# Three chunks of the merge gates as block products behind the recurrent branch, and one plain chunk between each two pairs of the branch

## The chip, the cores and the metric

The kernel runs on one NeuronCore of one Trainium2 chip. The metric is device time in microseconds (us), lower is better; a stated time is the median of several executions. A profile shows one execution. Its engines are TensorE (PE, matrix products), VectorE (DVE), ScalarE (ACT), GpSimd (POOL) and SyncE (SP), which here only issues loads. Each engine runs its instructions in order and waits on semaphores for the others.

## The reference

One layer of a streaming encoder: 512 frames of 1024 features, all in float32.

```python
xn = rmsnorm(h, norm_mix_g)
u = xn @ w_in                       # 1024 x 7168: q, k, v, xr, gr, ga, gb
ya = chunked_band_attention(q, k, v, rel_table) @ w_attn_out
xc = causal_depthwise_conv(xr, conv_w, conv_b)
hr = rg_lru(xc, w_r, b_r, w_i, b_i, lam)
yb = (hr * gelu(gr)) @ w_rnn_out
g_a, g_b = split(sigmoid(concat(ga, gb) + b_merge))
h = h + (g_a * ya + g_b * yb) @ w_o
h = h + SwiGLU(rmsnorm(h)); out = rmsnorm(h)
```

What matters here are the merge gate g_b = sigmoid(xn @ W_gb + b), 512 x 1024, and the branch's way out, yb.

## The kernel before, in words

**Products.** Every float32 operand is split into a high part (float32r) and the low rest; mm3 (L74) makes a product as three matmuls: high x high, high x low, low x high. Weights come in chunks of 256 columns (two tiles of 128 output features, c = 0 and 1). A plain chunk holds two half chunks of four k tiles each; project (L342) runs eight k of three matmuls over 512 frames for each c, that is 48 matmuls of 128 x 512. The weight is the stationary operand, and xn, turned so that features lie on partitions (xnT), moves past it.

**Chunks.** plan (L96) lists the chunks in the order of their use, `xr0 gr0 ga0 gb0 xr2 ...`. weights (L336) hands out a chunk and has prefetch (L308) load and split the ones ahead of it: load (L157) issues the load on SP into a "raw" buffer (three), ScalarE copies the high part (L82), VectorE subtracts it for the low part (L83), both into "whl" buffers (four, so two chunks).

**Block products.** Chunks named in `strassen` (in the feed-forward stage, from chunk 2 on) are multiplied in another form: weight_sums (L181) cuts the chunk in four blocks (two halves of k, two halves of the columns), forms four sums s1 to s4 of blocks on VectorE and splits a11, a12, (s2, s1), (s3, s4) and a22. block_product (L362) then does seven products of four k, over 256 frames each: a11 b11, a12 b21, s2 t2, s1 t1, s3 t3, s4 b22, a22 t4, where b are blocks of the moving side and t1 to t4 its sums. ScalarE keeps partial results (L370), VectorE adds them (L382, L383). That makes 84 matmuls of 128 x 256.

**The stage in question.** Pair by pair (j = 0, 2, 4, 6) the recurrent branch runs: xr, its conv (conv_in, conv_taps, conv_out), gr with GeLU, the small gate matmuls "rg" (L709), then a chain on ScalarE, VectorE and GpSimd (rnn_gates L715, rnn_scan L739) that ends with the tile rnn (L746, L747). Between pairs stand plain chunks of merge gates: after pairs 0 and 2 ga and gb, after 4 and 6 only gb. Each gate tile is half a tanh (L780). Then come q and k of head pair 0, v0 (four v_tile's), yb0 to yb6 (L968 to L972, multiplied into the gate zB), and the heads. The scores of head 0 are asked for before yb6. The heads (transposed, scores, weigh) are in a section whose TensorE order is written out by hand; there transposed turns the probabilities through two PSUM banks "t" and one "mm". PSUM has four banks "mm", two "s" and two "t"; the v tiles of v0 use "t".

**Order.** Outside sections with a manual schedule a list scheduler in the compiler orders each engine's instructions: ready ones first, in the order of the code. Pools of SBUF are stacked; a pool opened after another is closed lies on the same memory, and each of its tiles waits for the tiles that lay there. The branch's pools rw and rw2 are closed ahead of attention's aw2 and aw.

## Time and profile before

| what | value |
|---|---|
| median of 3 executions | 866.96 us (866.88 to 867.3) |
| the profiled execution | 867.3 us |
| its span, first to last instruction | 865.5 us |
| TensorE busy | 856.4 us (99%) |
| VectorE busy | 600.9 us (69%) |
| ScalarE busy | 498.1 us (58%) |
| GpSimd busy | 95.2 us (11%) |
| TensorE's granted clock | 0.998 of full |

"Busy" is the time in which an instruction of the engine ran. Matmuls overlap, so the rate is read from the distance between starts, not from their lengths. In a timeline row the columns are: start, duration, engine, line, operation, output and inputs, shapes, count, and in brackets the idle time before it with what ended it. In a row of groups: line, engine, operation, shapes, count, then total busy us, mean ns, and idle us before with what ended it.

### The profile page before, as it was taken

What the parts mean: (1) busy time and instruction counts of PE and PEld (TensorE: products, weight loads), DVE (VectorE), ACT (ScalarE), POOL (GpSimd) and SP (SyncE); (2) the same over time, 40 slices, a digit from 0 to 9 for tenths busy, and PEclk for the clock granted to TensorE, in tenths of its full rate; (3) what the DMA queues carried; (4) which work ended last, traced back from release to release, by engine and by line L of the source; (5) the groups of instructions that cost most, each with busy time, mean ns of one, the idle gap of its engine ahead of it and who ended that gap; (6) DMA issues with size and microseconds to landing.
All of it is one profiled execution on the core that took longest, in us unless ns stands there. A gap on an engine that the chain in (4) does not pass through costs nothing.

```text
span 865.5 us, 13353 instructions
## 1 busy us (share of the span) xinstructions
PE 856.4 (99%) x5130; PEld 761.1 (88%) x5130; DVE 600.9 (69%) x950; ACT 498.1 (58%) x878; POOL 95.2 (11%) x161
## 2 busy tenths in 40 slices
PE   9999999999999999999999999999999999999997
PEld 6988888888889889898888889999999999888885
DVE  5666656573456585766556556988888888698885
ACT  6595747752356585767633357555555556545434
POOL 2412111120112132221200000000000001000000
PEclk9999999999999999999999999999999999999999
DMA  9133232433323332232223712424333332437542
GB/s 289 57 119 106 68 120 76 123 98 98 109 88 95 81 103 74 81 113 64 74 76 121 266 51 72 145 79 131 109 98 98 99 98 85 148 100 227 185 134 97
DMA packets 88767, 96.39 MB, mean 111 GB/s; under 512 B 5784, under 2 KB 74992, under 8 KB 88704
## 3 DMA queue, kind: packets, MB, share of 16 engines
q1 hardware_dynamic: 87072, 92.03, 34.3%
q10 hardware_dynamic: 1232, 2.95, 0.9%
q8 instruction: 40, 0.66, 0.3%
q0 software_dynamic: 400, 0.57, 0.2%
q14 instruction: 23, 0.19, 0.1%
HBM read 93.39 MB, written 2.14 MB: 110 GB/s over the span
## 4 chain that ended last, share of the span: by engine, by line
PE 97%; DVE 1%; ACT 1%; DMA 0%; issue 0%; ACTq 0%; DVEq 0%
PE po_out L76 2%; PE po_out L77 2%; PE po_out L78 2%; PE o L941 2%; PE p_fu L78 2%; PE p_fg L78 2%; PE p_fg L77 2%; PE p_fg L76 2%; PE p_fu L76 2%; PE p_fu L77 2%; PE pT L921 2%; PE po_v L76 2%; PE po_v L78 2%; PE po_v L77 2%; PE po_gb L76 2%; PE po_xr L77 2%
## 5 line engine op out<-in xcount | busy, mean ns | idle before, releaser
L910 POOL TENSOR_SCALAR p<-p,rl 128x128 f32<-128x128 f32 (+3 forms) x61 | 34.9, 590 | 135.7 <-DVE rl L906 135.4
L905 ACT ACTIVATE p<-p,m 128x128 f32<-128x128 f32 (+1 forms) x64 | 35.7, 560 | 11.0 <-DVE m L904 10.8
L76 PE MATMUL po_v<-whl_v,xnT 128*128 128x256 f32 x128 | 36.5, 285 | 0.0
L78 PE MATMUL po_v<-whl_v,xnT 128*128 128x256 f32 x128 | 36.2, 283 | 0.0
L77 PE MATMUL po_v<-whl_v,xnT 128*128 128x256 f32 x128 | 36.2, 283 | 0.0
L1131 POOL TENSOR_TENSOR act_lo<-act,act_hi 128x1024 fp32r<-128x1024 f32 x1 | 2.4, 2405 | 300.7 <-ACT act_hi L1130 300.7
L76 PE MATMUL po_out<-whl_fo,act_hi 128*128 128x512 f32 (+1 forms) x80 | 30.8, 385 | 0.5 <-ACT c_u L370 0.5
L78 PE MATMUL po_out<-whl_fo,act_lo 128*128 128x512 f32 (+1 forms) x80 | 30.7, 384 | 0.0
L77 PE MATMUL po_out<-whl_fo,act_hi 128*128 128x512 f32 (+1 forms) x80 | 30.7, 384 | 0.0
L904 DVE CUSTOM_DVE_ANT_0 p<-s,bias 128x128 f32<-128x128 f32 (+1 forms) x64 | 29.1, 483 | 1.0 <-PE s L896 1.0
L83 DVE TENSOR_TENSOR whl_qk<-raw_qk,whl_qk 128x1024 fp32r<-128x1024 f32 x16 | 20.5, 1284 | 13.2 <-ACT whl_qk L82 13.0
L83 DVE TENSOR_TENSOR whl_fu_s<-s_fu,whl_fu_s 128x1024 fp32r<-128x1024 f32 x20 | 24.1, 1222 | 6.2 <-ACT whl_fu_s L82 6.2
L77 PE MATMUL po_xr<-xnT,whl_xr 128*128 128x512 f32 (+1 forms) x80 | 27.7, 353 | 0.0
L83 DVE TENSOR_TENSOR pp<-pT,pp 128x384 fp32r<-128x384 f32 (+1 forms) x48 | 27.5, 596 | 0.1
L77 PE MATMUL po_gr<-xnT,whl_gr 128*128 128x512 f32 (+1 forms) x80 | 27.5, 347 | 0.0
L78 PE MATMUL po_gr<-xnT,whl_gr 128*128 128x512 f32 (+1 forms) x80 | 27.3, 347 | 0.0
L78 PE MATMUL po_xr<-xnT,whl_xr 128*128 128x512 f32 (+1 forms) x80 | 27.2, 346 | 0.0
L76 PE MATMUL po_gr<-xnT,whl_gr 128*128 128x512 f32 (+1 forms) x80 | 27.2, 347 | 0.0
L83 DVE TENSOR_TENSOR whl_fg_s<-s_fg,whl_fg_s 128x1024 fp32r<-128x1024 f32 x20 | 24.0, 1222 | 4.1 <-ACT whl_fg_s L82 4.0
L76 PE MATMUL po_xr<-xnT,whl_xr 128*128 128x512 f32 (+1 forms) x80 | 26.3, 351 | 0.4 <-ACT xnT L566 0.4
L82 ACT ACTIVATE whl_qk<-raw_qk 128x1024 fp32r<-128x1024 f32 x16 | 16.8, 1053 | 17.0 <-PE po_yb L78 10.4
L76 PE MATMUL po_gb<-xnT,whl_gb 128*128 128x512 f32 x64 | 25.2, 394 | 0.0
(487 smaller groups left out, 3247.5 us busy)
## 6 DMA issues: line engine op xcount, KB each, us to landing
raw_fg<-in_w_ffn_in_dram SPq DMA_DIRECT2D x24, 512.0 KB, 4.2
raw_fu<-in_w_ffn_in_dram SPq DMA_DIRECT2D x22, 512.0 KB, 3.9
raw_qk<-in_w_in_dram SPq DMA_DIRECT2D x32, 256.0 KB, 3.2
raw_fo<-in_w_ffn_out_dram SPq DMA_DIRECT2D x16, 512.0 KB, 3.6
raw_xr<-in_w_in_dram SPq DMA_DIRECT2D x8, 512.0 KB, 4.3
raw_gr<-in_w_in_dram SPq DMA_DIRECT2D x8, 512.0 KB, 3.6
raw_ga<-in_w_in_dram SPq DMA_DIRECT2D x8, 512.0 KB, 4.7
raw_gb<-in_w_in_dram SPq DMA_DIRECT2D x8, 512.0 KB, 3.5
```

Of the source, the lines that this page charges most:

```text
L76: pe.matmul(o, sh, mh, start=start, stop=False, skip_group_check=parts)
L77: pe.matmul(o, sh, ml, start=False, stop=False, skip_group_check=parts)
L78: pe.matmul(o, sl, mh, start=False, stop=stop, skip_group_check=parts)
L82: act.activation(hi, src, AF.Copy)
L83: dve.tensor_sub(lo, src, f(hi))
L904: dve.tensor_tensor_reduce(prob[qb][:], scs[qb][:, 0:w], bias[:, S - w:S], -1.0, 3e38, ALU.add, ALU.min, nmax[:, qb:qb + 1])
L905: act.activation(prob[qb][:], prob[qb][:], AF.Exp, bias=nmax[:, qb:qb + 1], scale=-1.0, accum_out=lsum[:, qb:qb + 1])
L910: eng.tensor_scalar(prob[qb][:], prob[qb][:], rl[:, qb:qb + 1], 1.0, ALU.mult, ALU.mult)
L921: pe.transpose(pt[:, at * P:(at + 1) * P], prob[qb][:, kb * P:(kb + 1) * P], ident[:])
L941: pe.matmul(po[:, S - n:S], st, pp[i][:, part, lo:lo + n], start=kb == 0 and part == 0, stop=kb == NT - 1 and part == 1)
L1131: (dve if i else pool).tensor_sub(lo[:], o[:], f(hi[:]))
```

## The change

gb0, gb2 and gb4 are computed as block products, at a new place. The order of chunks between the branch's pairs becomes: ga0 after pair 0, ga2 after pair 2, q and k of head pair 0 after pair 4, gb6 after pair 6. Then: yb0, the sums t1 to t4 of xn (sums_of_x), yb2, gb0, yb4, gb2, gb4, yb6, and last v0 and the heads, with head 0's scores ahead of v0. yb0 to yb4 are copied to zB unmultiplied (way_out); block_gate puts its product in a tile of ta that is not yet used, applies the tanh there and multiplies into zB. A pool gs holds the sums between the closing of rw and rw2 and the opening of aw2 and aw; its first 32 KB for each partition are the split sums, then the place for sums in the making. The feed-forward stage keeps its own sums pool, and the counters are reset for it. The diff without the lines that only rename sums_room:

```diff
@@ -91,29 +91,29 @@
 
     chunks = []
     index = {}
-    strassen = [f"f{w}{j}" for j in range(2, FT, 2) for w in "gu"]
+    strassen = ["gb0", "gb2", "gb4"] + [f"f{w}{j}" for j in range(2, FT, 2) for w in "gu"]
 
     def plan(name, *parts, rows=0, kts=KT):
         index[name] = len(chunks)
         chunks.append((name, parts, rows, kts))
+
+    def plan_qk(pr):
+        plan(f"qk{pr}", cols(w_in, C_Q + pr * P, P), cols(w_in, C_K + pr * P, P))
 
     for j in range(0, KT, 2):
         plan(f"xr{j}", cols(w_in, C_XR + j * P))
         plan(f"gr{j}", cols(w_in, C_GR + j * P))
         if j < 4:
             plan(f"ga{j}", cols(w_in, C_GA + j * P))
-        plan(f"gb{j}", cols(w_in, C_GB + j * P))
-
-    def plan_qk(pr):
-        plan(f"qk{pr}", cols(w_in, C_Q + pr * P, P), cols(w_in, C_K + pr * P, P))
+        if j == 4:
+            plan_qk(0)
 
     def plan_v(gr):
         plan(f"v{gr}", cols(w_in, C_V + gr * CW))
 
-    plan_qk(0)
+    for name in ("gb6", "yb0", "yb2", "gb0", "yb4", "gb2", "gb4", "yb6"):
+        plan(name, cols(*((w_in, C_GB + int(name[2]) * P) if name[0] == "g" else (w_rnn_out, int(name[2]) * P))))
     plan_v(0)
-    for j in range(0, KT, 2):
-        plan(f"yb{j}", cols(w_rnn_out, j * P))
     for pr in range(1, HEADS // 2):
         plan_qk(pr)
         if pr in (2, 4, 6):
@@ -160,7 +160,7 @@
         n = min(4 * CW // wide, kts - k)
         at = rows + k * P
         pl, bufs = wp, 3
-        if name in strassen and name[0] == "f":
+        if name in strassen:
             loads[0] += 1
             pl, bufs = (room[0], 1) if loads[0] % 4 == 0 and loads[0] > 4 else (wp, 3)
         raw = pl.tile([P, n, wide], F32, tag="raw", bufs=bufs, name=f"raw_{name}_{k}")
@@ -465,7 +466,7 @@
     gm_p = ps.tile([P, S], F32, tag="s", bufs=2, name="gm_p")
     pe.transpose(gm_p[:, 0:8], gm_r[:], ident[0:8, 0:8])
     gm = cp.tile([P, 8], F32, name="gm")
-    _, xnT = features(xnp, "xn", "xnT")
+    xnT_all, xnT = features(xnp, "xn", "xnT")
 
 
     vc = cp.tile([P, NV], F32, name="vc")
@@ -794,26 +795,10 @@
         g = [gelu_in(0, po[0])]
         xch.append(conv_out(1, xc[1]))
         g.append(gelu_in(1, po[1]))
-        prefetch(index["gb0"] + 1)
+        prefetch(index["xr2"] + 1)
         for c in range(2):
             gelu_out(g[c], po[c])
             conv[c] = xc[c], xch[c], g[c]
-    for j in range(0, KT, 2):
-        if j:
-            for c in range(2):
-                conv[j + c] = rnn_conv(j + c, tile_of(f"xr{j}", c, ahead=2))
-        for c in range(2):
-            if j:
-                po = tile_of(f"gr{j}", c, "t")
-                conv[j + c] += (rnn_gelu(j + c, po),)
-        if j:
-            gates_of(j)
-        for w in range(j // 4, 2):
-            for c in range(2):
-                gate(w, j + c)
-            if j == w == 0:
-                gates_of(j)
-
 
     def blocks(ap):
         return ap.rearrange("p (b i) -> p b i", i=P)
@@ -855,10 +840,83 @@
             pool.tensor_copy(kl[other, e], kl[own, e])
         qk[pr] += [kh, kl]
 
-    q_tile(0)
-    k_tile(0)
+    for j in range(0, KT, 2):
+        if j:
+            for c in range(2):
+                conv[j + c] = rnn_conv(j + c, tile_of(f"xr{j}", c, ahead=2))
+            for c in range(2):
+                po = tile_of(f"gr{j}", c, "t")
+                conv[j + c] += (rnn_gelu(j + c, po),)
+            gates_of(j)
+        if j < 4:
+            for c in range(2):
+                gate(0, j + c)
+        elif j == 4:
+            q_tile(0)
+            k_tile(0)
+        else:
+            for c in range(2):
+                gate(1, j + c)
+        if j == 0:
+            gates_of(0)
+
     rw2_stack.close()
     rw_stack.close()
+
+    gs_stack, gs = opened("gs")
+    bt_homes = {i: gs.tile([P, 2, 4, 256], F32R, name=f"xt{i}") for i in (2, 1, 3, 4)}
+    sums_room[0] = room[0] = gs
+
+    def way_out(j):
+        for c in range(2):
+            po = mm_tile(f"po_yb{j + c}")
+            project(po, weights(f"yb{j}"), c, rnn)
+            act.activation(zB[j + c], po[:], AF.Copy)
+
+    def block_of_x(kh, half, part):
+        return xnT_all[:, 4 * kh:4 * kh + 4, part, half * 256:half * 256 + 256]
+
+    def sums_of_x():
+
+        x32 = gs.tile([P, 2, 4, 256], F32, tag="whl", name="x32")
+        x12, x22 = x32[:, 0], x32[:, 1]
+        t1, t2, t3, t4 = (gs.tile([P, 4, 256], F32, tag=tag, bufs=bufs, name=f"x_t{i + 1}")
+                          for i, (tag, bufs) in enumerate((("s21", 1), ("s34", 1), ("a22", 2), ("a22", 2))))
+        dve.tensor_add(x12, f(block_of_x(0, 1, 0)), f(block_of_x(0, 1, 1)))
+        dve.tensor_sub(t1[:], x12, f(block_of_x(0, 0, 0)))
+        dve.tensor_sub(t1[:], t1[:], f(block_of_x(0, 0, 1)))
+        dve.tensor_add(x22, f(block_of_x(1, 1, 0)), f(block_of_x(1, 1, 1)))
+        dve.tensor_sub(t2[:], x22, t1[:])
+        dve.tensor_sub(t3[:], x22, x12)
+        dve.tensor_sub(t4[:], f(block_of_x(1, 0, 0)), t2[:])
+        dve.tensor_add(t4[:], t4[:], f(block_of_x(1, 0, 1)))
+        for i, t in ((2, t2), (1, t1), (3, t3), (4, t4)):
+            split_pair(bt_homes[i], t[:])
+        return right_side(lambda kh, half, part, k: block_of_x(kh, half, part)[:, k], [bt_homes[i] for i in range(1, 5)])
+
+    def block_gate(j, n, x_right):
+
+
+        z, o = zs[0][2 + n % 2], zs[1][j // 2]
+        block_product(f"gb{j}", n % 2, x_right, z[:].rearrange("p a (b n) -> p (a b) n", n=256))
+        for c in range(2):
+            at = 24 + j + c
+            act.activation(z[:, c], z[:, c], AF.Tanh, bias=hb[:, at:at + 1], scale=0.5)
+        dve.scalar_tensor_tensor(o[:], z[:], 1.0, o[:], ALU.add, ALU.mult)
+
+    way_out(0)
+    x_right = sums_of_x()
+    way_out(2)
+    block_gate(0, 0, x_right)
+    way_out(4)
+    block_gate(2, 1, x_right)
+    block_gate(4, 0, x_right)
+
+    for j in (6, 7):
+        po = mm_tile(f"po_yb{j}")
+        project(po, weights("yb6"), j % 2, rnn)
+        dve.scalar_tensor_tensor(zB[j], zB[j], 1.0, po[:], ALU.add, ALU.mult)
+    gs_stack.close()
     aw2_stack, aw2 = opened("aw2", 2)
     aw_stack, aw = opened("aw", 2, "right")
 
@@ -961,15 +1019,9 @@
                 2: ([va(1), va(2)], [va(3)]),
                 3: ([qs(second)], [ks(second)])}[at]
 
+    prob = scores(0)
     for t in range(NT):
         v_tile(0, t)
-
-    for j in range(KT):
-        if j == 6:
-            prob = scores(0)
-        po = mm_tile(f"po_yb{j}")
-        project(po, weights(f"yb{j - j % 2}"), j % 2, rnn)
-        dve.scalar_tensor_tensor(zB[j], zB[j], 1.0, po[:], ALU.add, ALU.mult)
     with tc.manual_schedule(engines={mybir.EngineType.PE}):
         for h in range(HEADS):
             pp = transposed(h, prob)
@@ -1002,7 +1054,8 @@
 
     hp = ctx.enter_context(pool_of("h", 1, "right"))
 
-    sums_room = ctx.enter_context(pool_of("sums", 1, "right"))
+    sums_room[0] = ctx.enter_context(pool_of("sums", 1, "right"))
+    slots[0] = loads[0] = 0
     hn_stack, hnp = opened("hnT", 1, "right")
     ht = [hp.tile([P, D], F32, name=f"h{t}") for t in range(NT)]
     for t in range(NT):
@@ -1121,10 +1174,10 @@
         if i == 0:
             hi = acp.tile([P, 2, S], F32R, tag="act", bufs=13, name=f"act_hi{i}")
         elif i < 3:
-            hi = sums_room.tile([P, 2, S], F32R, tag=("s21", "s34")[i - 1], bufs=1, name=f"act_hi{i}")
+            hi = sums_room[0].tile([P, 2, S], F32R, tag=("s21", "s34")[i - 1], bufs=1, name=f"act_hi{i}")
         else:
             if i == 3:
-                hi_room.append(sums_room.tile([P, 2, 2, S], F32R, tag="whl", bufs=1, name="act_hi34"))
+                hi_room.append(sums_room[0].tile([P, 2, 2, S], F32R, tag="whl", bufs=1, name="act_hi34"))
             hi = hi_room[0][:, i - 3]
         lo = acp.tile([P, 2, S], F32R, tag="act", bufs=13, name=f"act_lo{i}")
         act.activation(hi[:], o[:], AF.Copy)
```

7 lines of the change are left out of this document (4 added, 3 removed).

## The prediction

> **What bounds the kernel now.** I read the page first: the engine shares, the granted clock, and the chain that ended last.
>
> ```profile
> span 865.5 us, 13353 instructions
> PE 856.4 (99%) x5130; PEld 761.1 (88%) x5130; DVE 600.9 (69%) x950; ACT 498.1 (58%) x878; POOL 95.2 (11%) x161
> ...
> PEclk9999999999999999999999999999999999999999
> ...
> PE 97%; DVE 1%; ACT 1%; DMA 0%; issue 0%; ACTq 0%; DVEq 0%
> ```
>
> TensorE is busy for 99% of the span at full clock, and 97% of the last chain is TensorE itself. So a change pays only by taking matmul time out, and it costs whatever makes TensorE wait. Busy shares hide the rate, because neighbouring matmuls overlap; the timeline gives start-to-start times. First, one chunk of merge gate as it is now, from its first matmul to the first one of the next chunk:
>
> ```profile
> 94.57 0.39 PE L76 MATMUL po_gb<-xnT,whl_gb 128*128 128x512 f32 x1
> ...
> 105.45 0.39 PE L76 MATMUL po_xr<-xnT,whl_xr 128*128 128x512 f32 x1
> ```
>
> The 48 matmuls (two halves, eight k, three each) of 512 columns take 10.88 us, 0.2267 us each. Second, a block product of the feed-forward stage, which has the shape that the gates are to get:
>
> ```profile
> 577.99 0.28 PE L76 MATMUL p_fg<-hn,whl_fg_a 128*128 128x256 f32 x1
> 578.11 0.28 PE L77 MATMUL p_fg<-hn,whl_fg_a 128*128 128x256 f32 x1
> 578.23 0.28 PE L78 MATMUL p_fg<-hn,whl_fg_a 128*128 128x256 f32 x1
> ```
>
> A matmul of 256 columns starts every 0.12 us, a little over half of 0.2267.
>
> **The change part by part.** *The matmuls.* A block product does seven products of four k and three matmuls: 84 x 0.12 = 10.08 us in place of 48 x 0.2267 = 10.88 us. That is 0.80 us less per chunk, and 2.4 us less for gb0, gb2 and gb4. All other matmuls stay and only move. The price per matmul decides: at 10.88 / 84 = 0.1295 us nothing would be gained, and the row shows 0.12.
>
> [...]
>
> *The new order.* gb0 and gb2 leave the branch, and qk0 takes the place of gb4 (24 + 24 matmuls of 512 columns, also 10.88 us). So everything from the last pair of the branch on comes two chunks, 21.76 us, earlier. Behind that pair now come gb6, yb0, yb2, gb0, yb4, gb2, gb4, yb6. The rows that matter are where TensorE is, and when the branch ends:
>
> ```profile
> 161.75 1.66 PE L709 MATMUL rg<-xch,wrg 64*128 64x512 f32 x12
> 163.34 0.50 PE L76 MATMUL po_gb<-xnT,whl_gb 128*128 128x512 f32 x1
> ```
>
> ```profile
> 182.05 1.26 DVE L742 SCALAR_TENSOR_TENSOR u<-u,g 128x512 f32<-128x512 f32 x2
> ...
> 183.53 2.55 POOL L747 TENSOR_TENSOR rnn<-u,rnn 128x512 fp32r<-128x512 f32 x2 [8.71 <-ACT rnn L746]
> ```
>
> The last gate matmuls of the branch (rg) start at 161.75, gb6 at 163.34; the two last rnn tiles are written by 186.08, the first of them at about 184.8. Shifted: gb6 starts at 141.58 and ends at 152.46, the rnn tiles are there at 163.0 and 164.3. Before, gb6, qk0 and v0 covered this; now yb0 follows gb6 and needs rnn6 for its seventh k. If TensorE kept strictly to the order of the code, it would run 18 matmuls (4.08 us, to 156.5) and then stand for 6.5 us. But the first six k of the four tiles of yb0 and yb2 are 72 matmuls or 16.3 us, which reach to 168.8. That the schedule does bring such matmuls forward is seen in the profile of before:
>
> ```profile
> 190.86 0.28 PE L78 MATMUL po_v<-whl_v,xnT 128*128 128x256 f32 x1
> 190.98 0.40 PE L76 MATMUL po_yb<-rnn,whl_yb 128*128 128x512 f32 x1
> ...
> 192.59 0.28 PE L76 MATMUL po_v<-whl_v,xnT 128*128 128x256 f32 x1
> ```
>
> Seven matmuls of yb stand between two of the v tiles, taken forward because v had no bank. The four tiles need four "mm" banks, and there are four. I cost this at nothing, with 4.5 us to spare; without that cover it costs 6.5 us.
>
> *The sums, on VectorE.* gb0's first two products need only raw blocks and x. The third, s2 with t2, needs sums of both. gb0 starts two chunks after gb6's end, at 174.2; 24 matmuls later, at 177.1, s2 and t2 must be there. From 141.6 that is 35.5 us. What VectorE has to do by then, priced by these rows:
>
> ```profile
> L83 DVE TENSOR_TENSOR whl_fg_s<-s_fg,whl_fg_s 128x1024 fp32r<-128x1024 f32 x20 | 24.0, 1222 | 4.1 <-ACT whl_fg_s L82 4.0
> L83 DVE TENSOR_TENSOR whl_fg_a<-raw_fg,whl_fg_a 128x512 fp32r<-128x512 f32 x30 | 20.3, 684 | 1.1 <-ACT whl_fg_a L82 1.0
> L1146 DVE TENSOR_TENSOR act<-act,c_u 128x1024 f32<-128x1024 f32 x10 | 12.2, 1219 | 0.3 <-ACT c_u L370 0.3
> L741 DVE TENSOR_TENSOR_SCAN u<-a,gt 128x512 f32<-128x512 f32 x8 | 9.3, 1208 | 0.0
> L195 DVE TENSOR_TENSOR s_fg<-raw_fg,raw_fg 128x512 f32<-128x512 f32 x10 | 6.9, 687 | 0.2 <-DMA raw_fg<-in_w_ffn_in_dram 0.2
> L735 DVE SCALAR_TENSOR_TENSOR u<-u 128x512 f32<-128x512 f32 x8 | 5.8, 732 | 0.5 <-POOL a L733 0.5
> L731 DVE SCALAR_TENSOR_TENSOR u<-gt,u 128x512 f32<-128x512 f32 x8 | 5.6, 698 | 8.0 <-ACT gt L729 8.0
> L736 DVE SCALAR_TENSOR_TENSOR gt<-gt,xc 128x512 f32<-128x512 f32 x8 | 5.5, 693 | 14.0 <-ACT gt L721 14.0
> L697 DVE SCALAR_TENSOR_TENSOR g<-g,po_gr 128x512 f32<-128x512 f32 x8 | 5.5, 686 | 2.7 <-ACT g L696 2.7
> L740 DVE SCALAR_TENSOR_TENSOR gt<-gt,u 128x512 f32<-128x512 f32 x8 | 5.2, 688 | 3.0 <-ACT u L759 3.0
> L742 DVE SCALAR_TENSOR_TENSOR u<-u,g 128x512 f32<-128x512 f32 x8 | 5.2, 675 | 0.0
> ```
>
> The branch's last pair: 2 x (0.693 + 0.698 + 0.732 + 0.688 + 1.208 + 0.675) = 9.4, and 1.4 for what is left of its GeLU. Weights of yb0 and yb2: 4 x 1.22 = 4.9. Sums of x: eight of 1024 elements at 1.22 = 9.8. The low parts of the four sums: 4 x 1.22 = 4.9. gb0: four sums at 0.69, two halves at 0.68 and one pair at 1.22 = 5.3. Together 35.7 us in 35.5 us; 30.8 if the low parts of t3 and t4 are left for later and the first two sums, whose tile lies over no tile of the branch, are done before 141.6. How full VectorE can be while TensorE never waits is seen here:
>
> ```profile
> core 0: us, PE busy (x) PEld busy (x) DVE busy (x) ACT busy (x) POOL busy (x), PEclk, DMA share, GB/s
> ...
> 163.30:185.00 21.70, 21.70 (x98) 17.95 (x96) 14.30 (x18) 17.09 (x25) 3.38 (x6) 1.00 0.41 122
> ...
> 549.00:749.00 200.00, 200.00 (x1653) 199.31 (x1653) 163.47 (x220) 116.99 (x207) 2.40 (x1) 1.00 0.34 106
> ```
>
> In the feed-forward stage VectorE is at 82% with no loss. The need here is 87% (30.8 of 35.5). Bounds: nothing, if the holes of 7.4 us beside the branch (14.3 busy of 21.7) are filled with sums of x (a gain there is excluded, since TensorE has no hole to give back); at 82% the short list takes 37.6 us and is 2.1 late, the full one 43.5 and 8.0 late. Nearest is the 82% row, without a loss: I take 0 and keep 8.0. ScalarE (17.1 of 21.7 us) also has four copies of x sums, the gate's splits and four copies of yb there; it has the same deadline, and a delay there is in the same bounds.
>
> Behind gb0 the products run as in the feed-forward stage, with yb4 and yb6 between them that need only two splits each: cost 0. The added tanh and the product on z lie beside them.
>
> *The memory.* The pools of attention now open behind gb4, so the loads of bias rows queue on SP behind that release, and the loads of qk1 behind them. yb6's 10.88 us lie between: cost 0, and about 1 us if the load is late.
>
> *The end of the stage.* Before, yb6 and yb7 lie between v0 and head 0's transposes. Now the v tiles do. The v tiles and pT0, pT1 share the two "t" banks, and TensorE's order is fixed from head 0 on. So pT1 waits until the fourth v tile has left its bank:
>
> ```profile
> 195.34 0.28 PE L78 MATMUL po_v<-whl_v,xnT 128*128 128x256 f32 x1
> ...
> 195.66 0.38 ACT L82 ACTIVATE v<-po_v 128x256 fp32r<-128x256 f32 x1 [4.10 <-PE po_v L78]
> ...
> 196.08 0.42 DVE L83 TENSOR_TENSOR v<-po_v,v 128x256 fp32r<-128x256 f32 x1 [4.06 <-ACT v L82]
> ```
>
> ```profile
> 229.43 0.22 PE L895 MATMUL s<-kh,q 128*128 128x128 f32 x1
> ...
> 241.60 1.25 PE L921 MATMUL pT<-ident,p 128*128 128x128 f32 x10
> ```
>
> From the last matmul's start to the end of the emptying it is 196.50 - 195.34 = 1.16 us when both engines are free. One v matmul and the four transposes of pT0 (0.11 each, from ten in about 1.1 us) cover 0.12 + 0.44 of it. What is left is 0.6 us; with ScalarE or VectorE in the midst of a 1.2 us split it is up to 1.8; it is 0 if other work stands there. I take 0.6. The softmax of head 0 has as long as before: 12.2 us from scores to transposes in the row, 1.1 + 11.5 (96 v matmuls of 0.12) after.
>
> *The first pairs.* With gb0 gone, xr2 follows the first rg at once. If its conv is late for the second rg, ga2 can run first, another 10.88 us of ready matmuls: 0.
>
> *The sum:* -2.4 + 0.6 = -1.8 us. The profiled execution took 867.3 us, of which 865.5 are the span, so it would become 865.5 (span 863.7). It lay 0.34 us over the median of 866.96; on the median that makes **865.2**.
>
> **The rivals.** *Clean.* Other matmuls or an earlier emptying hide the wait at pT1: -2.4, 864.6. For it: the profile of before shows hardly a hole in TensorE.
>
> *VectorE late.* The sums of x don't fit into the holes of the branch, because their tiles come free late or because the branch's own steps go first. Place: the third product of gb0. Against it: 82% without loss in the feed-forward stage; for it: a need of 87% to 100%. Price 0 to 8.0 on top of my sum, 2.1 by the short list: 865.2 to 873.2, nearest 867.3. It decides for slower from 3.5 us of lateness on (1.8 to eat the gain, 1.7 for the bound).
>
> *yb0 waits for the branch.* TensorE stands 6.5 us at the seventh k of yb0: 871.7. For it: three chunks of cover become one. Against it: the seven matmuls brought forward. It decides from the point where weights of yb2 or a free bank are missing at 160.6, when yb0's first six k are done.
>
> *The change doesn't do what it says:* block products among plain chunks run at over 0.1295 us a matmul, so that no time leaves TensorE. The feed-forward row is against it. At 0.14 they lose 84 x 0.0105 x 3 = 2.6 instead of gaining 2.4: 870.2. [...]
>
> **How the numbers follow.** My forecast, with its own range of 864.8 to 866.0 from the bounds at pT1 and small waits, has 0.40; clean 0.17; VectorE late 0.27; yb0 waiting 0.12; matmul price 0.04. 0.2% is 1.7 us, about what a measurement of this kernel can tell from no change; the border to faster is 865.2, the middle of my forecast. So faster gets 0.17 and half of 0.40 and a little of late VectorE: 0.40. Within 0.2% (865.2 to 868.7): 0.20 and half of late VectorE: 0.32. Slower: the rest of it, 0.12 and 0.04: 0.28. The range 864.4 to 870.4 leaves out yb0's wait and the worst of late VectorE, under 0.2.
>
> **What would show it.** Right: no p_gb matmul over 0.12 us apart; three block products of 10.1 us; a hole of 0.6 us at head 0's second transpose; yb2's matmuls ahead of yb0's seventh k. Wrong: a hole of TensorE before s2 of gb0 that ends on VectorE (whl_gb, or a sum of x), or one in yb0 that ends on POOL's rnn; a branch whose rg comes later than 21.8 us before its old place; loads of bias landing after head 0's scores.

## The result, and the profile after

The changed kernel takes 879.09 us (median of 4 runs, 878.36 to 879.64) against 866.95 before (866.88 to 867.3). The ratio is 1.0139, with a 95% interval of 1.0121 to 1.0156: it is slower by 12.1 us. The forecast was 865.2, with a range of 864.4 to 870.4 and a chance of 0.28 for slower, so both the sign and the size were wrong. The profiled execution took 878.82 us, of which 877.0 are the span; before, the span was 865.5.

First the page of the kernel after, for the same rows as before:

```profile
span 877.0 us, 13638 instructions
PE 859.1 (98%) x5238; PEld 766.3 (87%) x5238; DVE 630.4 (72%) x986; ACT 514.4 (59%) x912; POOL 105.6 (12%) x161
...
PEclk9999999899999999999999999999999999999999
...
PE 80%; ACT 8%; DVE 8%; issue 1%; DMA 1%; POOL 1%; SPq 0%; ACTq 0%; DVEq 0%
```

TensorE's share of the last chain has fallen from 97% to 80%, and one of the 40 slices shows a lower granted clock. TensorE's busy time has even grown, by 2.7 us, although it has less work: a matmul of 512 columns at half clock counts as busy for 0.63 us instead of 0.39. So busy time can't be used for the account. I use the distances between starts of neighbouring matmuls instead: each distance is compared with the usual one of that shape (the median over both profiles: 0.227 us for 512 columns, 0.12 for 256 and so on), and what is over is a loss.

| part of the span | before: loss, us | after: loss, us |
|---|---|---|
| 0 to 60 us (normalization, first pair) | 5.2 | 5.2 |
| 60 to 80 (gates of pair 2) | 0.0 | 2.7 |
| 80 to 160 | 0.8 | 0.8 |
| 160 to 180 (yb after, pair 6's gates before) | 0.4 | 7.3 |
| 180 to 200 (gb0 after) | 0.0 | 3.2 |
| 200 to 240 | 0.0 | 0.1 |
| 240 to 260 (head 0 after) | 0.0 | 1.1 |
| the rest | 1.1 | 1.1 |
| all losses | 7.5 | 21.4 |
| usual distances of all matmuls | 850.3 | 847.8 |

Each pair's gate products lose 0.4 us in both kernels, at other places of the span; pair 2's stand at 60 to 80 us after, so its new loss is 2.3. The matmuls are 2.45 us cheaper and the losses are 13.96 us dearer, which gives the 11.5 us of the span. What TensorE waited for at each place stands in the waits of the kernel after, between 60 and 260 us (columns: waiting line, what it waited for, us in all, times, the longest):

```profile
PE po_yb L77 <- POOL rnn L748: 4.3, 1, 4.3
PE p_gb L76 <- ACT whl_gb_s L82: 2.1, 1, 2.1
PE rg L710 <- ACT xch L680: 1.6, 1, 1.6
PE pT L979 <- DVE v L83: 0.9, 1, 0.9
PE p_gb L78 <- DVE whl_gb_s L83: 0.5, 1, 0.5
```

The reader should see four places. All four had been named by the prediction, at costs of 0, 0, 0 and 0.6 us. The two waits named p_gb belong to one place, the block product gb0. The largest loss, at yb, is more than its wait, as the windows around it show:

```profile
core 0: us, PE busy (x) PEld busy (x) DVE busy (x) ACT busy (x) POOL busy (x), PEclk, DMA share, GB/s
167.50:172.00 4.50, 0.22 (x2) 0.01 (x1) 4.47 (x4) 0.00 (x0) 4.50 (x2) 0.89 0.00 0
172.00:177.50 5.50, 5.50 (x13) 4.34 (x14) 1.14 (x2) 1.70 (x3) 2.16 (x1) 0.50 0.01 3
```

TensorE stands still for 4.4 us, and then the granted clock is 0.50: 13 matmuls in 5.5 us, 0.42 us each instead of 0.2267. The clock fell at 171.0, still within the stop; until it is full again at 177.8 it adds 2.9 us. During the stop GpSimd is busy all the time, and with a single subtraction. This is the timeline of GpSimd and then of VectorE there:

```profile
165.34 8.81 POOL L748 TENSOR_TENSOR rnn<-u,rnn 128x512 fp32r<-128x512 f32 x2 [8.01 <-ACT rnn L747]
```

```profile
163.87 1.27 DVE L743 SCALAR_TENSOR_TENSOR u<-u,g 128x512 f32<-128x512 f32 x2
165.05 1.22 DVE L885 TENSOR_TENSOR x<-xnT 128x1024 f32<-128x1024 f32 x1
166.19 1.22 DVE L888 TENSOR_TENSOR x<-xnT 128x1024 f32<-128x1024 f32 x1
...
169.59 1.22 DVE L887 TENSOR_TENSOR x_t<-x_t,xnT 128x1024 f32<-128x1024 f32 x1
170.85 2.17 DVE L889 TENSOR_TENSOR x_t<-x,x_t 128x1024 f32<-128x1024 f32 x1
```

Before, GpSimd's two low parts of rnn6 and rnn7 took 2.55 us together; now they take 8.81 (6.59 and then 2.26). From 165.05 on VectorE runs the sums of x without a gap, each starting before the one ahead of it has ended, at their usual 1.22 us. The first of them starts before the last scan step (L743) has ended. GpSimd doesn't get on until VectorE's row has its first gap, at 170.81. The branch itself is late by little: its last L743 ends at 165.14, where the old place less 21.76 us is 161.55. Of these 3.6 us 2.3 are pair 2's loss, which TensorE has too; the chain from the last gate products to the scans' end is 1.3 us longer than before.

Last, the block product where nothing holds it up:

```profile
196.75 0.28 PE L76 MATMUL q_gb<-xnT,whl_gb_s 128*128 128x256 f32 x1
196.87 0.28 PE L77 MATMUL q_gb<-xnT,whl_gb_s 128*128 128x256 f32 x1
196.99 0.28 PE L78 MATMUL q_gb<-xnT,whl_gb_s 128*128 128x256 f32 x1
```

The matmuls are 0.12 us apart, as in the feed-forward stage.

### The profile page after: what moved, and what is told of

Same layout as the page of the kernel before. It is cut to its first block, busy times and chain, and to the rows that moved or that the text cites. A ratio compares the mean times of both kernels' runs of the same rounds, so it can differ in the third digit from the quotient of the medians.

```text
span 877.0 us, 13638 instructions
## 1 busy us (share of the span) xinstructions
PE 859.1 (98%) x5238; PEld 766.3 (87%) x5238; DVE 630.4 (72%) x986; ACT 514.4 (59%) x912; POOL 105.6 (12%) x161
## 4 chain that ended last, share of the span: by engine, by line
PE 80%; ACT 8%; DVE 8%; issue 1%; DMA 1%; POOL 1%; SPq 0%; ACTq 0%; DVEq 0%
ACT gt L722 2%; PE po_out L76 2%; PE po_out L77 2%; PE po_out L78 2%; PE o L999 2%; PE p_fu L78 2%; PE p_fg L78 2%; PE p_fg L77 2%; PE p_fg L76 2%; PE p_fu L76 2%; PE p_fu L77 2%; PE pT L979 2%; DVE xc L676 2%; PE po_v L76 2%; PE po_v L78 2%; PE po_v L77 2%
## 5 line engine op out<-in xcount | busy, mean ns | idle before, releaser
L77 PE MATMUL po_yb<-rnn,whl_yb 128*128 128x512 f32 x64 | 26.3, 412 | 4.3 <-POOL rnn L748 4.3
L76 PE MATMUL po_gr<-xnT,whl_gr 128*128 128x512 f32 (+1 forms) x80 | 27.1, 347 | 0.0
L78 PE MATMUL po_yb<-rnn,whl_yb 128*128 128x512 f32 x64 | 26.1, 409 | 0.0
```

The source lines that it names most:

```text
L76: pe.matmul(o, sh, mh, start=start, stop=False, skip_group_check=parts)
L77: pe.matmul(o, sh, ml, start=False, stop=False, skip_group_check=parts)
L78: pe.matmul(o, sl, mh, start=False, stop=stop, skip_group_check=parts)
```

## The experiments

The theory after this reading: the matmul saving is real, and most of the 14 us (yb's 7.3 and gb0's 3.2) come from VectorE. It has no free stretch of 9.8 us for the eight sums of x; and where they run in an unbroken row, they shut GpSimd out, so that the branch's last low parts are late. The rivals: GpSimd is slow for another reason (its own operands, memory), or TensorE is late because of ScalarE or of the loads. The runs below ask three things. Is it the shutting out? What is its rule? And what is left of the loss if the sums stand elsewhere?

### What made GpSimd late

**The low parts on VectorE.** The one line that runs on GpSimd goes to VectorE for the last pair.

```diff
-        pool.tensor_sub(o[:, 1], u, f(o[:, 0]))
+        (dve if j >= 6 else pool).tensor_sub(o[:, 1], u, f(o[:, 0]))
```

> The changed kernel, but the low parts of the last two rnn tiles are made by VectorE instead of GpSimd. Theory A (GpSimd is shut out of SBUF while VectorE runs its sums of x one after the other): the hole of 4.4 us in yb and the 2.9 us at half clock behind it go, rnn's low parts are there about 3 us after the scan; 879.1 - 7.3 = 871.8, or up to 4 us more if VectorE's queue then ends the wait for s2 of gb0 later. Rival B (the branch itself is late and GpSimd only carries the delay on): the hole in yb stays at about 4 us and the time stays near 879.

Measured: 876.94 us, ratio 1.0118 (1.0101 to 1.0134), span 874.2. The waits of TensorE from 25 to 260 us:

```profile
PE p_gb L76 <- ACT whl_gb_s L82: 3.2, 1, 3.2
PE rg L710 <- ACT xch L680: 1.7, 1, 1.7
PE p_gb L78 <- DVE whl_gb_a L83: 1.5, 1, 1.5
...
```

The wait at yb is gone and so is its half clock (mean granted clock 0.997 instead of 0.994). But gb0 now waits longer and in more places: it loses 7.7 us where it lost 3.2 in the change. So of yb's 7.3 us 2.8 were saved and the rest came back. Theory A was right on the wait at yb; the time lies 1.1 us above the 875.8 that it allowed at most. In this run VectorE works from the scans to 186.2 us with no gap over 0.4 us, and gb0's weight parts come last. That is VectorE out of time (it also has the two low parts now), which the long stop at yb had hidden: while TensorE stood there, the sums ran.

**Additions put into the kernel before.** Six additions of 128x1024 from two SBUF tiles go behind pair 2's scans and six reductions with one input behind pair 6's; nothing uses them.

```diff
         while held:
             rnn.append(rnn_scan(*held.pop(0)))
+        for n in range(6):
+            if j == 2:
+                dve.tensor_add(zs[0][2][:], u_pairs[-1][:], f(xnT_all[:, 0]))
+            if j == 6:
+                q = cp.tile([P, 2], F32, tag="hsq2", bufs=2, name=f"dummy{n}")
+                dve.tensor_reduce(q[:], u_pairs[-1][:], mybir.AxisListType.X, ALU.add)
```

> The kernel before, with six additions of 128x1024 from two SBUF inputs put on VectorE right behind the last scan of pair 2, and six reductions of 128x1024 (one SBUF input) behind the last scan of pair 6; their results are not used. Theory A: GpSimd's first low part of rnn in pair 2 grows from 1.3 to 6 us or more, the one in pair 6 stays at 1.3. Rival B (any dense stretch of VectorE, or ScalarE's or DMA traffic, slows GpSimd): both grow, or neither. Time: 867 to 870.

Measured: 867.12 us, span 865.4. Beside the additions the two low parts take 2.22 and 2.29 us, beside the reductions 1.30 and 1.31 as ever. So the additions with two SBUF inputs slowed GpSimd here, and the reductions with one did not. But they took turns: GpSimd waited for one addition and VectorE for one low part (the second addition took 2.2 us). Theory A's 6 us or more are not there.

**The same additions to two tiles in turn**, so that none needs the one ahead of it.

```diff
+                dve.tensor_add(zs[0][2 + n % 2][:], u_pairs[-1][:], f(xnT_all[:, n % 4]))
```

> The kernel before with the six additions of 128x1024 behind pair 2's last scan again, now written by turns to two tiles, so that no addition waits for the one ahead of it. Theory A (VectorE instructions with two SBUF inputs keep GpSimd out until VectorE has a gap): GpSimd's first low part of rnn in pair 2 takes 4 us or more, against 2.2 us where the additions followed each other into one tile. Rival B (whoever comes first has its turn, then the other): 2.2 us again. Time 867 to 868.

Measured: 867.05 us, low parts of 2.20 and 2.28 us. They took turns again although VectorE's instructions overlapped. That a row without gaps is enough to shut GpSimd out was wrong in this form.

**Twelve additions of 512** that read the first half of u.

```diff
+                dve.tensor_add(zs[0][2 + n % 2][:, n // 2 % 2], u_pairs[-1][:, 0], f(xnT_all[:, n % 8, 0]))
```

> The kernel before with twelve additions of 128x512, each with two SBUF inputs, put behind pair 2's scans (their results are overwritten and used by nothing). Theory C (GpSimd is shut out as long as VectorE's two-input instructions follow one another without a gap): the low part L747 of pair 2 takes 4 us or more instead of 1.30. Rival D (they take turns, as with the additions of 1024): the two low parts take 1.6 to 2.3 us each, and VectorE's additions beside them are stretched by as much. The time stays within 0.1% of before, for nothing there is on the path.

Measured: 867.31 us. The timeline of GpSimd and of VectorE:

```profile
103.66 10.44 POOL L747 TENSOR_TENSOR rnn<-u,rnn 128x512 fp32r<-128x512 f32 x1 [8.52 <-ACT rnn L746]
```

```profile
102.77 0.69 DVE L742 SCALAR_TENSOR_TENSOR u<-u,g 128x512 f32<-128x512 f32 x1
103.37 0.69 DVE L764 TENSOR_TENSOR za<-u,xnT 128x512 f32<-128x512 f32 x1
...
111.13 1.22 DVE L83 TENSOR_TENSOR whl_gr<-raw_gr,whl_gr 128x1024 fp32r<-128x1024 f32 x1
112.27 0.69 DVE L764 TENSOR_TENSOR za<-u,xnT 128x512 f32<-128x512 f32 x1
112.87 1.53 DVE L675 SCALAR_TENSOR_TENSOR xc<-po_xr,vc,xc 128x511 f32<-128x511 f32 x2
```

One subtraction took 10.44 us. GpSimd was shut out through fourteen instructions and got on when L675 came, whose input is a PSUM tile. So a delay like the change's 6.59 us can be made in the kernel before. What differs from the run before is open: width, form of the operands, or the start. In this run the first addition starts at 103.37, ahead of L742's end (102.77 + 0.69 = 103.46), since it reads only the half of u that was done already; in the two runs before it started 0.03 to 0.04 us behind that end.

**Strided and flat additions of 1024 that read only x.** Both are held back by copies of one column of u. The two runs ask whether the form of the operands decides. The first addition in the lines below is that of the strided run, the second that of the flat run.

```diff
+                dve.tensor_copy(zs[0][2 + n][:, 0, 0:1], u_pairs[-1][:, 0, 0:1])
...
+                dve.tensor_add(zs[0][2 + n % 2][:].rearrange("p a (b n) -> p (a b) n", n=256), f(xnT_all[:, 0:4, 0, 256:512]), f(xnT_all[:, 0:4, 1, 256:512]))
...
+                dve.tensor_add(zs[0][2 + n % 2][:], f(xnT_all[:, n]), f(xnT_all[:, n + 1]))
```

> The kernel before with six additions of 128x1024 behind pair 2's scans, each reading two strided stretches of x's parts as the change's sums do (results used by nothing). [...]

> The same with six additions that read two flat stretches of 1024 of x's parts and nothing of the branch. [...] Rival D (what let GpSimd in was that the additions read the same tile u as the low parts, or came with a gap behind the scans): 4 us or more.

Measured: 867.27 and 867.22 us; low parts of 2.27 us, all four of them. Strided reads alone didn't shut GpSimd out, and additions that read nothing of the branch let it in as well, so the form of the operands doesn't decide. In both runs the row has no gap ahead of it, but two copies with one input.

**Width against gap.** Two runs cross them: additions of 1024 without a gap ahead of their row (two of 512 that read the first half of u go first, as shown), and the twelve additions of 512 with one (they read `u_pairs[-1][:, 1]`, the second half, instead of `[:, 0]`).

```diff
+                dve.tensor_add(zs[0][2 + n][:, 0], u_pairs[-1][:, 0], f(xnT_all[:, n, 0]))
...
+                dve.tensor_add(zs[0][2 + n % 2][:], f(xnT_all[:, n]), f(xnT_all[:, n + 1]))
```

> As the flat additions of 1024 in the kernel before, but what holds them back is two additions of 128x512 that read only the first half of pair 2's u, so they begin before the last scan step L742 has ended, as in the change and in the twelve additions of 512. Theory G (what decides is whether VectorE's row of two-input instructions was already under way, one overlapping the next, when GpSimd's request came: then GpSimd stays out until the row breaks; if the request falls in the first instruction behind a gap, it gets in at that one's end): the first low part L747 takes 4 us or more. Rival H (additions of 1024 let GpSimd in, those of 512 do not): it gets in behind the first or second addition of 1024, 2.5 to 3.7 us, and the second takes 2.2 us.

> The twelve additions of 512 again, but reading the second half of u, so the first of them begins only behind the end of the last scan step L742, with a gap of about 0.04 us as the additions of 1024 had. Theory G: GpSimd gets in at the end of the first addition and they take turns, low parts of 1.6 to 1.9 us. Rival H: shut out again, about 10 us.

Measured: 867.09 and 867.05 us. GpSimd with additions of 1024 and no gap (the first addition starts at 103.27, L742 ends at 103.36):

```profile
103.56 11.24 POOL L747 TENSOR_TENSOR rnn<-u,rnn 128x512 fp32r<-128x512 f32 x1 [8.75 <-ACT rnn L746]
```

and VectorE and GpSimd with additions of 512 behind a gap:

```profile
102.53 0.69 DVE L742 SCALAR_TENSOR_TENSOR u<-u,g 128x512 f32<-128x512 f32 x1
103.25 0.69 DVE L764 TENSOR_TENSOR za<-u,xnT 128x512 f32<-128x512 f32 x1
```

```profile
103.42 1.67 POOL L747 TENSOR_TENSOR rnn<-u,rnn 128x512 fp32r<-128x512 f32 x1 [8.76 <-ACT rnn L746]
```

The only difference between 10.44 and 1.67 us is which half of the u tile the additions read: with the second half the first of them begins at 103.25, 0.03 us behind L742's end at 103.22. With 1024 the same two cases took 11.24 us and 2.20 to 2.29, so width doesn't decide between them. That the additions read the half that the low part reads isn't the reason either: the sums of the change read nothing of u, and GpSimd was shut out all the same.

The rule as the runs show it: GpSimd's request came each time during the first instruction behind the scan steps. If that one had begun before the last scan step ended, GpSimd stayed out until VectorE's row of two-input instructions broke (low parts of 5.59 to 11.24 us). If it began 0.03 to 0.04 us behind that end, or behind copies with one input, GpSimd got on at its end, and from then on they took turns (1.30 to 2.29 us). Other gaps and other moments of the request were not tried.

**The gap in the change itself.** Two copies of one column wait for ScalarE's rounded rnn6 and stand ahead of the sums.

```diff
+        for at in (x12, x22):
+            dve.tensor_copy(at[:, 0, 0:1], f(rnn[6][:, 0, 0:1]))
         dve.tensor_add(x12, f(block_of_x(0, 1, 0)), f(block_of_x(0, 1, 1)))
```

> The kernel after with one thing more: two copies of one column wait for the rounded rnn6 and stand ahead of the sums of x, so that VectorE's row of two-input instructions is broken once, behind the scans. Theory G: GpSimd's low part of rnn6 takes its turn with the sums, 1.3 to 2.4 us instead of 6.59, both low parts are done near 169 to 170 us instead of 174.2, the hole of 4.44 us ahead of yb's last products shrinks to under 2.5 us and brings no half clock (about 5 us saved), and the sums, 2 to 3 us later, add as much at gb0: span 873 to 875, about where the low parts on VectorE came out (874.2). Rival H (the row of the sums shuts GpSimd out in any case): the hole stays at 4 us or more, span 877 or above.

Measured: 877.73 us, ratio 1.0118 (1.0102 to 1.0135), span 877.0. The low parts take 1.30 and 2.27 us, and no wait at yb is left among TensorE's waits:

```profile
PE p_gb L76 <- ACT whl_gb_s L82: 3.2, 1, 3.2
PE p_gb L78 <- DVE whl_gb_a L83: 2.0, 1, 2.0
PE rg L710 <- ACT xch L680: 1.6, 1, 1.6
```

The loss at yb falls from 7.3 us to nothing, and the one at gb0 rises from 3.2 to 9.2, together 1.3 us less. In the profiled execution this is eaten by pair 2, where a hole of the same 1.9 us was followed by half clock (4.3 us instead of 2.7). The mechanism is what theory G said: with the row broken GpSimd isn't shut out. The span of 873 to 875 was missed, because gb0 took back more than was set down for it, and because of pair 2. So curing yb alone takes only 1.4 us (here) or 2.2 us (low parts on VectorE) off the time; VectorE's lateness for gb0 comes out behind it.

### Where the sums can stand

**Early.** The sums' tiles are taken from the gate tiles that are still unused, and the schedule moves them ahead to 25.5 to 38.8 us.

```diff
-        x32 = gs.tile([P, 2, 4, 256], F32, tag="whl", name="x32")
...
+        x12, x22, t1, t2 = (z[:].rearrange("p a (b n) -> p (a b) n", n=256)
+                            for z in (zs[0][2], zs[0][3], zs[1][1], zs[1][2]))
```

> The changed kernel, but the sums of x are made in gate tiles that are not yet in use, instead of in the pool that is opened over the branch's memory. Theory A says the sums then fill holes of VectorE early, GpSimd's low part of rnn6 falls from 6.6 us to 1.3 to 3 us, the hole in yb and the half clock behind it go, and the wait for s2 of gb0 goes as well: 879.1 - 7.3 - 2.9 = 868.9. Rival B (scheduler keeps the order of the code whatever the memory): the sums stay behind the last scan, 879. Rival C (VectorE has too much to do in that stretch, wherever the sums stand): the waits move ahead into the branch, 875 to 879.

Measured: 879.84 us, ratio 1.0144 (1.0129 to 1.0159). Waits of TensorE:

```profile
PE po_ga L78 <- DVE whl_ga L83: 3.5, 1, 3.5
PE po_yb L77 <- POOL rnn L748: 3.3, 1, 3.3
```

gb0's waits are gone; ga0's weights are late in their place. Theory A's 868.9 was missed by 11 us; rival B is out as well, since the place of the tiles did move the sums, and the new wait is the kind that rival C named. And yb still waits: behind the scans VectorE now runs gb0's own sums and the low parts of x's sums in a row, and GpSimd's low part takes 5.59 us. So a row of other two-input instructions does it too, not these sums alone.

**v0 ahead of yb6**, for the wait at pT1 alone.

```diff
-    for name in ("gb6", "yb0", "yb2", "gb0", "yb4", "gb2", "gb4", "yb6"):
+    for name in ("gb6", "yb0", "yb2", "gb0", "yb4", "gb2", "gb4"):
...
     plan_v(0)
+    plan("yb6", cols(w_rnn_out, 6 * P))
```

> The changed kernel, but v0 and head 0's scores come ahead of yb6, as before the change. Theory (the fourth v tile has to leave its bank before the second transpose of head 0): the hole of 1.0 us at that transpose goes, 878.0. Rival: another wait, such as the load of bias or head 0's softmax, takes its place, 879 or more.

Measured: 879.61 us, ratio 1.0141 (1.0125 to 1.0156), span 875.9. The loss between 240 and 260 us goes from 1.14 to 0.03, and the span falls by 1.1. The timed runs don't show it: they spread over 2.7 us, with a mean clock of 0.992 to 0.995 from run to run.

**Cures together.** The sums in gate tiles, held back by a copy of one column of pair 2's u; the low parts on VectorE; then v0 ahead of yb6 as well; then gb0 plain again, between pairs 0 and 2 (blocks gb2 and gb4 only).

```diff
+        for at in (x12, x22):
+            dve.tensor_copy(at[:, 0, 0:1], u_pairs[1][:, 0, 0:1])
...
-    strassen = ["gb0", "gb2", "gb4"] + [f"f{w}{j}" for j in range(2, FT, 2) for w in "gu"]
+    strassen = ["gb2", "gb4"] + [f"f{w}{j}" for j in range(2, FT, 2) for w in "gu"]
```

> The changed kernel with both: low parts of the last two rnn tiles on VectorE, and the sums of x made in gate tiles, held back until pair 2's scans are over. Theory A (GpSimd shut out, and behind that a VectorE that is late because the sums start behind the last scan): the hole in yb and the waits of gb0's s2 both go, 879.1 - 7.3 - 3.2 = 868.6. Rival C (VectorE has too much to do wherever the sums stand): the branch's gate matmuls come later, 872 to 877.

> As the run with both cures, and v0 and head 0's scores ahead of yb6 as before the change. Theory: 1.0 us less than with both cures, 867.6. Rival: the transposes' hole is replaced by another wait, same as with both cures.

> As the run before this one, and gb0 stays a plain chunk between pair 0 and pair 2, so that only gb2 and gb4 are block products. Theory: the wait of 2.1 us at the gate matmuls of pair 2 goes with the chunk back between the pairs; the second saving is 0.8 us smaller: 867.6 - 2.1 + 0.8 = 866.3, and if TensorE then has no hole left the kernel is at 867.1 - 1.6 = 865.5. Rival: a VectorE that is too full keeps a hole of over 2 us somewhere, 868 or more.

Measured: 875.68 us (ratio 1.0093, 1.0078 to 1.0108), 873.6 (1.0072, 1.0055 to 1.0089) and 871.42 (1.0049, 1.0034 to 1.0064); spans 874.1, 871.8 and 869.1. From 160 to 200 us nothing is lost in any of the three, and with v0 first nothing at head 0. But the times lie 5.1 to 7.1 us above what the theories gave. In each run a new loss stands at pair 4's gates: 7.0, 7.2 and 6.5 us are lost between 80 and 160, where the change lost 0.8. So for the first and the third run the rivals were right, by which a VectorE with too much to do only moves the wait. With gb0 back between the pairs the loss at pair 2 (2.8 us in the second run) is gone. What is left in the last one stands in one row of waits:

```profile
PE rg L713 <- ACT xch L683: 2.9, 1, 2.9
```

Pair 4's gates wait, with half clock behind it (mean 0.996): 5.6 us in all between 100 and 140. The cause is on VectorE again:

```profile
103.22 0.74 DVE L679 SCALAR_TENSOR_TENSOR xc<-po_xr,vc,xc 128x511 f32<-128x511 f32 x1
103.87 0.14 DVE L892 COPY za<-u 128x1 f32<-128x1 f32 x1
103.93 1.89 DVE L893 TENSOR_TENSOR za<-xnT 128x1024 f32<-128x1024 f32 x1
105.75 0.73 DVE L679 SCALAR_TENSOR_TENSOR xc<-po_xr,vc,xc 128x510 f32<-128x510 f32 x1
106.41 1.66 DVE L896 TENSOR_TENSOR za<-xnT 128x1024 f32<-128x1024 f32 x1
```

The conv's second and third step (L679) stand behind sums. GpSimd's low part of xch took 1.43 us there, so it isn't shut out: here it is VectorE's own order. The next run, in which the sums stand elsewhere and pair 4 waits no more, bears that out.

**In pair 6's gaps.** The copy that holds the sums back waits for pair 6's first GeLU. The first run has two blocks, the second all three; both keep the low parts on VectorE and v0 ahead of yb6. The edit is shown against the cures above.

```diff
-            dve.tensor_copy(at[:, 0, 0:1], u_pairs[1][:, 0, 0:1])
+            dve.tensor_copy(at[:, 0, 0:1], g_last[0][:, 0:1])
```

> The last cure alone is moved: as the kernel with two blocks (871.4 us, span 869.1), but the sums of x are released by pair 6's first gelu instead of pair 2's scans, so they stand between pair 6's gate steps, where VectorE of that run stood idle 9 to 10 us in pieces between 153 and 172 us. Theory A (the block products lose only because VectorE and GpSimd have no free stretch for the sums where they were put): pair 4's gate products come in time again, the hole of 3.2 us there and the half clock behind it (about 2 us) are gone, nothing new opens, span about 864 and time about 866. Rival B (the pieces are too short: each sum of 1.2 us delays a gate step, the scans end 3 us or more later, and gb2's weight parts behind them are late): a hole of 2 to 4 us at gb2's first products near 190 us, perhaps with half clock, time 868 to 871.

> The same place for the sums with all three block products as in the change (gb0 too, no plain gb0 between pairs 0 and 2). Theory A: beside the two-block kernel it saves another 0.8 us of matmul (28 x 0.12 against 16 x 0.2267 less per chunk), and loses what pair 2's gate products wait without gb0's cover, a hole of 1.8 to 2.2 us at 72 us as in the change itself: about 1.2 us more than the two-block kernel, 867. Rival B: 869 to 873, with holes at gb0's first products near 180 us as well.

Measured: 868.67 us, ratio 1.0017 (1.0008 to 1.0026), span 866.4; with three blocks 869.65 us, ratio 1.003 (1.0021 to 1.004), span 867.5. The waits of the first:

```profile
PE po_yb L76 <- ACT rnn L750: 1.1, 1, 1.1
PE p_gb L76 <- ACT keepa_gb L374: 0.8, 1, 0.8
```

Pair 4 is in time, and of the 12.1 us by which the change was slower all but 1.5 are gone, by all cures together. Neither expectation fits whole: the sums between the gate steps delay the scans by 3.4 us (from the first GeLU step L696 to the scans' end it is 27.1 us, in the two-block run above 23.7), as rival B said, but what TensorE waits for it at yb is 1.1 us, without half clock (mean 0.999). With three blocks pair 2's wait comes back (2.5 us more are lost there than with the chunk between) and outweighs the 0.8 us of the third block.

**The last two sums behind the scans.**

```diff
+        dve.tensor_copy(x12[:, 0, 0:1], u_pairs[3][:, 1, 0:1])
         dve.tensor_sub(x12, f(block_of_x(1, 0, 0)), t2)
```

> As the kernel with two blocks and the sums in pair 6's gaps (868.7 us, span 866.4), but the last two of the eight sums stand behind pair 6's scans, so the scans start about 2.3 us earlier. Theory A (what is left of its loss is VectorE's order and nothing else): the hole of 1.24 us at yb's products for rnn6 is gone, gb2's holes stay (0.9 us there, a DMA's), span 865.2, time 867.4, level with before. Rival B (VectorE's tail is as long as before and only moves the wait): the 1.24 us come back at gb2's weight parts, span 866.4.

Measured: 867.5 us, ratio 1.0005 (0.9996 to 1.0014), span 865.6. One wait is left:

```profile
PE q_gb L78 <- DVE whl_gb_s L83: 0.8, 1, 0.8
```

yb's hole is gone, and a wait of 0.8 us at gb2's weight parts stands in its place, which is the shift that rival B named; the second wait of the run before is gone too, and the time is near the 867.4 of theory A. This version is level with the kernel before; none was faster. Its matmuls are 1.63 us cheaper than before (two blocks) and its losses 0.9 us higher, and TensorE's last matmul does start 0.8 us earlier (858.06 against 858.84). The span of its profiled execution doesn't show this: from that matmul to the end it took 0.9 us longer, and the last store's issue-to-landing time was 3.4 us instead of 2.5.

## Why the prediction was wrong, by its own steps

**The matmuls** (-2.4 us): right. The account gives -2.45, and the rows show 0.12 us per matmul. The price rival falls.

**yb0 waits for the branch** ("I cost this at nothing, with 4.5 us to spare"): this is the step that failed with the largest loss, 7.3 us. Two things in it were wrong.

The first is the time of GpSimd's low part. The scans came only 1.3 us later than I had set down, besides the 2.3 us by which the whole stage was late. But the 1.3 us of the low part were taken from a profile in which VectorE beside it only ran a step with a PSUM input (L842); beside the sums it took 6.59. I had put the sums and the low part on two engines and added up each engine by itself. That the shut-out makes the wait is shown by the low parts on VectorE and by the two small copies ahead of the sums: both take yb's wait away.

The second is the cover, "72 matmuls" of four tiles. TensorE ran from 154.85 to 167.5 without a break, but only 56 matmuls: the first six k of three tiles, 54, and two of rnn6's high part. The fourth tile's 24 stood behind the wait. The copies of the finished tiles show it. The first three come 1.4 us apart from 175.81 on, and the fourth 5.4 us later, which is the time of its 24 matmuls:

```profile
177.25 0.59 ACT L874 ACTIVATE zb<-po_yb 128x512 f32<-128x512 f32 x1
178.67 0.60 ACT L874 ACTIVATE zb<-po_yb 128x512 f32<-128x512 f32 x1
184.12 0.60 ACT L874 ACTIVATE zb<-po_yb 128x512 f32<-128x512 f32 x1 [2.34 <-PE po_yb L78]
```

Its weights were split by 160.1, and the last gate tile ahead of it, gb6's second, had been read out of its bank by 157.1. So 18 of the 24 (4.1 us) look ready when TensorE stopped; standing ahead of the wait they would have taken it down to about 0.3 us, by an estimate from these starts. No run changed that order, so this half isn't tested, nor is it known why the schedule put the tile there. The rival's price of 6.5 us came near the loss by luck: its cause (missing banks or weights) is not what the trace shows. The half clock behind the stop was in neither.

**The sums, on VectorE** ("I take 0 and keep 8.0"): failed too. In the change gb0 lost 3.2 us, but only because TensorE already stood at yb; without that stop it lost 7.7 us (low parts on VectorE) or 9.2 (the gap in the change), half clock included; the far end that I had kept was 8.0. The step in it that failed: I counted the first two sums as done ahead of the last pair's gate steps and the holes between these steps as filled with sums. The schedule put all eight behind the last scan, although VectorE had 7.3 us free in the 23.55 us ahead of them (16.29 busy):

```profile
141.50:165.05 23.55, 23.55 (x109) 18.97 (x108) 16.29 (x20) 19.06 (x26) 2.64 (x3) 1.00 0.29 90
```

The holes that I meant to fill were real. Putting the sums into them by hand gained 4.0 us with three blocks and 2.8 with two, against the same kernels with the sums behind pair 2's scans; the rest of what was won back came from the other cures. Why the schedule left the holes unused is not shown beyond this: with the sums' tiles in the unused gate tiles it put the sums early by itself, so the place of their tiles decides, although I had taken the first two sums' tile to be free. In the change the wait at yb also made gb0 later by way of ScalarE, whose copies of yb stood ahead of the copies of x's sums in its queue:

```profile
164.63 1.18 ACT L747 ACTIVATE rnn<-u 128x512 fp32r<-128x512 f32 x2 [4.25 <-DVE u L743]
175.81 0.60 ACT L874 ACTIVATE zb<-po_yb 128x512 f32<-128x512 f32 x1 [10.00 <-PE po_yb L78]
176.30 1.05 ACT L82 ACTIVATE xt<-x_t 128x1024 fp32r<-128x1024 f32 x1
```

ScalarE stood for 10 us behind a copy that waited for TensorE, while the sums that it had to round were ready from 169.7 (t3) to 173.0 (t2) on.

**The first pairs** (0): failed, 2.3 us. xr2 does follow the first rg at once, and its conv is late for the second rg as feared; but ga2 did not run first, because the second rg stood ahead of it in TensorE's order. One plain chunk between the two pairs takes the loss away (two blocks: 0.0 from 60 to 80 us).

**pT1** (0.6 us): right in place and mechanism, 1.1 in size. With v0 ahead of yb6 it is gone.

**Bias loads** (0): right; none of TensorE's waits goes back to them. GpSimd, which has little else to do there, does wait for them: 64.3 us in three waits, the last one up to 247 us.

So of 14.0 us of new losses 7.3 were at yb (4.4 of standing still and 2.9 of half clock), 3.2 at gb0, 2.3 at pair 2 and 1.1 at pT1. Three of the forecast's zeros (yb0, gb0, the first pairs) were argued from work or free time that would hide the step. Each time it was there, but the order of the engine that had to run it left it unused; none was checked for that.

## What to carry to other kernels

A step that is hidden costs nothing only if the order on the engine that runs it lets it be hidden: ask for each cover where the step will stand in that engine's row, not only how many free microseconds the row has. The saving of 2.4 us on a TensorE that was 99% busy was smaller than any one of the nine holes of 3.2 to 4.5 us in these profiles, and each of them had half clock behind it, for 1.6 to 3 us more. Count the holes first. When VectorE gets long rows of two-input work, in which a GpSimd step took 6.59 us here instead of 1.30, move the small GpSimd steps beside them that something waits for, or break the row just ahead of them, and count what VectorE then still has to do.

## What the runs showed of the hardware

**VectorE and GpSimd.** A subtraction of 128x512 on GpSimd took 1.30 us in the kernel before (the median of eight), 1.67 to 2.3 us in turns with VectorE's two-input instructions, and 5.59 to 11.24 us when it came while these were already overlapping. Beside reductions with one input it took 1.30 and 1.31 us, and the subtraction of 10.44 us ended 1.23 us after L675, which reads a PSUM tile, had started. In that run GpSimd was kept out through fourteen instructions, in a row whose first one started 0.09 us ahead of the scan's end. A gap of 0.03 us in that place made it 1.67 us, and copies with one input ahead of the row left it at 2.27. What the two engines contend for is not shown by these runs.

**The granted clock.** In the kernel after, the clock was at 0.50 from 171.0 to 177.8 us, behind the stop that began at 167.5: the hole of 4.4 us was followed by 5.7 us of matmuls 0.427 us apart instead of 0.227. Half clock stood behind each of the nine holes of 3.2 to 4.5 us (waits of 2.9 to 4.3 us). The mean clock of the eight profiles that have them is 0.992 to 0.997; that of the kernel before and of the three last versions, with no wait over 1.7 us, is 0.998 or 0.999. Shorter holes mostly left it alone: the hole of 1.9 us at pair 2 cost 2.7 to 2.9 us in five profiles, without half clock, and 4.3 in two, with half clock behind it. What sets these two apart from the five is not shown.
